# Transposing x for the last residual in the gap before the second norm, and reading the spread norm from PSUM

## The chip, the cores and the metric

The kernel runs on one core of a Trainium2 chip. The metric is the device time of one execution in microseconds (us). Three runs of the kernel before gave 1666.32, 1663.96 and 1669.1 us, so the median is 1666.32 us.

## The reference

One layer of a hybrid backbone works on 512 tokens of width 1024. What matters here lies between the two halves of the layer:

```python
    y, _ = bidir_mix(feats, lg_f, lg_b, ctx_states)
    x = x + g1 * (y.astype(x.dtype) @ w_out)
    x = x + g2 * peer_ffn(modulate(rmsnorm(x, norm2_w), sh2, sc2),
                          peer_w_q, peer_k1, peer_k2, peer_down, peer_up)
    ...
    return rmsnorm(x, norm_f_w)
```

`rmsnorm` divides each token by the root of its mean square, and `modulate` scales and shifts it. `peer_ffn` projects the result h to queries, multiplies them with two sets of 128 keys per head, takes the top 16 of each, the top 16 of their sums, and weights 16 expert rows per head. The x in front of `peer_ffn` is needed twice: for h, and at the very end, where the expert sum is added to it.

## The kernel before, in words

Up to the second norm x is held transposed: `xT` has the width on the partitions, as 8 tiles of 128 by 512 tokens. The attention half ends with the output projection (L641 to L649): TensorE (PE) makes eight PSUM tiles `px`, four at a time, and VectorE (DVE) adds each to `xT` (L650). ScalarE (ACT) squares each result, and DVE adds the squares up into `acc2`, except the last one, which stays alone as `sq` (L651 to L657).

Then comes the norm, with little for PE to do. `meansq` (L176) sums the squares over the partitions by twelve matmuls with one column each, the last four of which need `sq`. `rstd` (L199) takes the root on ACT (`r2`), the reciprocal on DVE, and `spread` makes a diagonal matrix `dg` on DVE and multiplies it with ones on PE, so that PSUM tile `rb` holds the factor of each token on every partition. ACT copies `rb` into the SBUF tile `rs2` (L204).

After that the pools of the first half are closed (`front.close()`), and pools of the second half take their SBUF and their eight PSUM banks. The loop at L684 makes h for each of the eight `xT` tiles: `tmp` = xT * a2x * rs2 on DVE, `hh` = tmp + shift rounded on ACT, `hl` = the rest on DVE, and `hg`, the last 128 tokens unrounded, on ACT. `tmp` has two buffers. `hg` is transposed on PE into `phr` and copied by ACT to `hr` (L691 to L696).

All later products are made by `product` (L698) in three matmuls per tile (`mm3`, lines L73 to L75): of rounded and rest parts. A weight block comes by DMA on SP's queue (`qr` or `dr`), is rounded on ACT (`qh`, `dh`), its rest is made on DVE (`ql`, `dl`), and 24 matmuls follow, into `pq` for a query block (L782) or into `pa` for a block of expert weights (L712). Expert blocks fill PE during the top-k loop (L791): a query block, the scores `pks` (L801), then three or four expert blocks for each half of a head, while DVE finds the maxima. Each of the eight heads ends with one piece of the transposition of `xT`: four PE transposes into `px2`, an ACT copy to `xr`, and a DMA to `x2d` in DRAM (L854 to L859). `finish` (L1021) reads `x2d` at the end of the kernel.

The order in which instructions stand on an engine is made by a scheduler from the program's dependences and its own costs. Each engine then works strictly through its own list. A tile that gets the memory of a closed pool waits until the instructions that still use that memory are done; this holds for PSUM banks and SBUF, and a buffer that a DMA reads is in use until the DMA has landed.

Of the kernel before, what the change touches and what calls it, by code (L numbers as in the profile page):

```python
# [9 lines left out]
F32 = mybir.dt.float32  # L10
# [4 lines left out]
AF = mybir.ActivationFunctionType  # L15
# [3 lines left out]
P = 128  # L19
D = 1024  # L20
KT = 8
L = 512
# [25 lines left out]
def body(nc, tc, a, out, dbg=None):  # L48
    V, S, G, T, Y = nc.vector, nc.scalar, nc.gpsimd, nc.tensor, nc.sync
# [3 lines left out]
    def pool(name, bufs=1, **kw):  # L53
        return tc.tile_pool(name=name, bufs=bufs, **kw)

    def open_pool(name, bufs=1, **kw):
        return es.enter_context(pool(name, bufs, **kw))

    cst = open_pool("cst")
# [5 lines left out]
    def ps(name, tag="ps"):  # L65
        return psum.tile([P, 512], F32, tag=tag, name=name, bufs=banks[tag])
# [17 lines left out]
    ident = cst.tile([P, P], F32, name="ident")  # L84
# [22 lines left out]
    wk = front.enter_context(pool("wk", 2))  # L107
# [4 lines left out]
    def tmp_tile(name, n=L):  # L112
        return wk.tile([P, n], F32, tag="t", name=name, bufs=4)
# [62 lines left out]
    def meansq(pt, terms):  # L176

        nc_ = terms[0].shape[-1] // P
        for i, sq in enumerate(terms):
            for c in range(nc_):  # L180
                T.matmul(pt[:, c:c + 1], sq[:, c * P:(c + 1) * P], onesd, start=(i == 0 and c == 0),
                         stop=(i == len(terms) - 1 and c == nc_ - 1))
# [5 lines left out]
    def inverse_rms(r, pt):  # L188
        S.activation(r, pt[:, :r.shape[-1]], AF.Sqrt, bias=epsc)
        V.reciprocal(r, r)  # L190

    def spread(pb, r, dg):

        nc_ = r.shape[-1]
        V.tensor_tensor(dg.rearrange("p (c j) -> p c j", j=P), ident[:, None, :].to_broadcast([P, nc_, P]),
                        r[:, :, None].to_broadcast([P, nc_, P]), MUL)
        T.matmul(pb[:, :nc_ * P], ones, dg, start=True, stop=True)

    def rstd(dst, pt, pb, dg, name):  # L199
        n = dst.shape[-1]  # L200
        r = cst.tile([P, n // P], F32, name=name)
        inverse_rms(r, pt)
        spread(pb, r, dg)
        S.activation(dst, pb[:, :n], AF.Copy)  # L204
        return dst
# [69 lines left out]
    def group(g, transposed, ctx_cols=None):  # L275
        px, pc = group_start(ctx_cols)
        for kp in range(4):
            group_piece(g, kp, px, pc, transposed, ctx_cols)
            mods_step(2)
        return px, pc  # L280
# [5 lines left out]
    px = [ps(f"px{i}", "px") for i in range(4)]  # L286

    pc2 = ps("pc", "pc")
    pc = [pc2[:, :256], pc2[:, 256:]]
# [123 lines left out]
    px, pc = group(1, False, (0, 512))  # L413
# [35 lines left out]
    for pr in range(2):  # L449
# [9 lines left out]
        for d in range(2):  # L459
# [22 lines left out]
            kn = wk.tile([P, 4, P], F32, name="kn")  # L482
# [61 lines left out]
    px, pc = group(2, True, (0, 512))  # L544
# [6 lines left out]
    px, pc = group(3, False, (0, 512))  # L551
# [13 lines left out]
    px, pc = group(4, True)  # L565
# [21 lines left out]
    for h in range(4):  # L587
# [9 lines left out]
        for b in range(4):  # L597
            psc = ps("psc", "pc")
            T.matmul(psc, rkT[:, h, b * P:(b + 1) * P], rqT[:, h], start=True, stop=True)
            pt = tmp_tile("pt")  # L600
# [5 lines left out]
    for g, tag in ((5, "gqk"), (6, "gv")):  # L606
        gt = mx.tile([P, 4, L], F32, tag=tag, name="gate")
        px, _ = group(g, True)
# [12 lines left out]
    for g, th, tl in ((0, "hch", "hcl"), (1, "hxh", "hxl")):  # L621
        yh = fe.tile([P, 4, L], F32R, tag=th, name="yh")
        yl = fe.tile([P, 4, L], F32R, tag=tl, name="yl")
        for i in range(4):
            h = 4 + i if g == 0 else i
# [9 lines left out]
    x2p = x2s.enter_context(pool("x2p", side="right"))  # L635
    x2d = drp.tile([L // P, P, D], F32, name="x2d")
    xT = x2p.tile([P, KT, L], F32, name="xT")
    Y.dma_start(xT, a["xT"])
    rs2 = x2p.tile([P, L], F32, name="rs2")
    sqs = []  # L640
    for dh in range(2):  # L641
        px = [ps(f"px{i}", "px" if dh else "pc" if i < 2 else "ps") for i in range(4)]
# [5 lines left out]
        for i in range(4):  # L648
            k = 4 * dh + i  # L649
# [8 lines left out]
    show("x2", xT)  # L658
    pt2 = ps("ms2")
    meansq(pt2, sqs)  # L660
    rstd(rs2, pt2, ps("rb"), tmp_tile("dg"), "r2")
    front.close()
    psa = open_pool("psa", space=bass.MemoryType.PSUM)
    pss = ExitStack()
# [16 lines left out]
    tw = qs.enter_context(pool("tw", 2))  # L681
# [10 lines left out]
    for i in range(2):  # L692
        pt = ps("phr", "b")
# [72 lines left out]
    def rows_step(n):  # L766
        for _ in range(n):
            next(rowwise, None)
# [22 lines left out]
    for h in range(H):  # L791
        vv = tw.tile([P, 2, 4, 16], F32, name="vv")
        vi = tw.tile([P, 2, 4, 16], U32, name="vi")
        for half in range(2):
            blk = 2 * h + half
            if blk + 1 < 2 * H:
                query(blk + 1)
            qT = qTs[blk]
            psc = ps("pks", "b")
            for t in range(4):  # L800
                T.matmul(psc[:, t * P:(t + 1) * P], qT[:, t * P:(t + 1) * P], keys[:, blk], start=True, stop=True)  # L801
            sc_ = tw.tile([P, 4, P], F32, name="sc_")
            S.activation(sc_, psc.rearrange("p (t n) -> p t n", t=4), AF.Copy)
            for t in range(4):
                if t < AHEAD[blk]:
                    ahead(1)
                if h:
                    rows_step(DOTS_H // 8)
                s2 = tw.tile([P, P], F32, name="s2")
                V.max(vv[:, half, t, 0:8], sc_[:, t])  # L810
                V.max_index(vi[:, half, t, 0:8], vv[:, half, t, 0:8], sc_[:, t])
                V.match_replace(s2, vv[:, half, t, 0:8], sc_[:, t], NEG)
                V.max(vv[:, half, t, 8:16], s2)
                V.max_index(vi[:, half, t, 8:16], vv[:, half, t, 8:16], s2)
        fi = tw.tile([P, 2, 4, 16], F32, name="fi")
        G.tensor_scalar_mul(fi[:, 0], vi[:, 0], 128.0)
        G.tensor_copy(fi[:, 1], vi[:, 1])
        cs = tw.tile([P, 4, NCAND], F32, name="cs")
        ce = tw.tile([P, 4, NCAND + NC8], F32, name="ce")
        for src, dst, rows in ((vv, cs, ROWS), (fi, ce, ROWS + tuple((r[0], r[1], r[2], NCAND + r[3]) for r in ROWS8))):  # L820
            for a0, na, nb, off in rows:
                o = dst[:, :, off:off + na * nb].rearrange("p t (x y) -> p t x y", x=na)
                G.tensor_tensor(o, src[:, 0, :, a0:a0 + na][:, :, :, None].to_broadcast([P, 4, na, nb]),
                                src[:, 1, :, 0:nb][:, :, None, :].to_broadcast([P, 4, na, nb]), ADD)
        tv = gall[:, :, h]
        ti = tw.tile([P, 4, 16], U32, name="ti")
        for t in range(4):
            s3 = tw.tile([P, NCAND], F32, name="s3")
            V.max(tv[:, t, 0:8], cs[:, t])
            V.max_index(ti[:, t, 0:8], tv[:, t, 0:8], cs[:, t])  # L830
            V.match_replace(s3, tv[:, t, 0:8], cs[:, t], NEG)
            V.max(tv[:, t, 8:16], s3)
            V.max_index(ti[:, t, 8:16], tv[:, t, 8:16], s3)
        G.tensor_tensor(ex[:, :, h], tv, tv[:, :, 0:1].to_broadcast([P, 4, 16]), SUB)
        if h == H - 1:
            S.activation(ex, ex, AF.Exp)

        tf = tw.tile([P, 2, 32, 2], F16, name="tf")
        for half in range(2):
            V.tensor_copy(tf[:, half].rearrange("p (t k) q -> p t k q", t=4),  # L840
                          ti[:, :, 8 * half:8 * half + 8][:, :, :, None].to_broadcast([P, 4, 8, 2]))
        for half, (c0, nc_) in enumerate(((NCAND, NC8), (0, NCAND))):
            ks = slice(8 * half, 8 * half + 8)
            eq = tw.tile([P, 32 * NCAND], F16, name="eq")[:, :32 * nc_]
            V.tensor_tensor(eq.rearrange("p (k c q) -> p k c q", k=32, q=2),
                            ic[:, c0:c0 + nc_].rearrange("p (c q) -> p c q", q=2)[:, None].to_broadcast([P, 32, nc_ // 2, 2]),
                            tf[:, half, :, None, :].to_broadcast([P, 32, nc_ // 2, 2]), ALU.is_equal)
            pe = tw.tile([P, 32 * NCAND], F32, name="pe")[:, :32 * nc_]
            V.tensor_tensor(pe.rearrange("p (t k c) -> p t k c", t=4, k=8), eq.rearrange("p (t k c) -> p t k c", t=4, k=8),
                            ce[:, :, c0:c0 + nc_][:, :, None, :].to_broadcast([P, 4, 8, nc_]), MUL)  # L850
            V.tensor_reduce(eall[:, :, h, ks], pe.rearrange("p (t k c) -> p t k c", t=4, k=8), AX.X, ADD)  # L851
        V.tensor_copy(rows_e[:, 16 * h:16 * h + 16], eall[:, 3, h])

        pt = ps("px2", "b")  # L854
        for k in range(4):
            T.transpose(pt[:, k * P:(k + 1) * P], xT[:, 4 * (h % 2) + k, (h // 2) * P:(h // 2) * P + P], ident)
        xr = tw.tile([P, 512], F32, name="xr")
        S.activation(xr, pt, AF.Copy)
        Y.dma_start(x2d[h // 2, :, 512 * (h % 2):512 * (h % 2) + 512], xr)  # L859
    zs = tq.tile([P, 4, H], F32, name="zs")  # L860
    V.tensor_reduce(zs, ex, AX.X, ADD)
    V.reciprocal(zs, zs)
# [14 lines left out]
    for src, dst in ((eall, eT), (gall, gT)):  # L877
        pt = ps("ptr", "b")[:, :NT]
# [165 lines left out]
    for j in range(NB // 2):  # L1044
        steps = pair_steps(j + 1) if j + 1 < NB // 2 else iter(())
        us, wh, wl = ready.pop(j)
        for x in range(2):
            uh, ul = us[x]
            i = 2 * j + x
            for tt in range(NT // P):  # L1050
# [6 lines left out]
                if j < len(due) and (x or tt):  # L1057
                    k = int(np.ceil((due[j] - done) / (6 - 3 * x - tt)))
# [93 lines left out]
```

## Time and profile before

| | us |
|---|---|
| median of three runs | 1666.32 |
| profiled execution | 1667.1 |
| its span, first to last instruction | 1665.3 |
| PE busy (97% of the span) | 1612.3 |
| DVE busy (76%) | 1272.5 |
| ACT busy (38%) | 633.1 |

The profiled execution's own time is 1.8 us over its span. The page shows the share of each engine, but the stretch of the change is only some 45 of 1665 us. It is read in the timeline of each engine, from 397 us (the end of the output projection) to 442 us (the end of the second set of scores).

### The profile page before, as it was taken

Reading aid. Unit: us, or ns where it says so; the run is one execution under the profiler, and the core shown is the slowest. Engines: PE = TensorE matmul, PEld = TensorE weight load, DVE = VectorE, ACT = ScalarE, POOL = GpSimd, SP = SyncE. Lnnn points to the kernel's source line nnn. Section 1 sums busy time; section 2 is a strip of 40 time slices with the busy share of each in tenths; the row PEclk is TensorE's granted clock in tenths of the full one; section 3 lists DMA queues with packets and bytes.
Section 4 is the critical chain, followed back from the end, with each engine's and each line's share of the span. In section 5 each row is a group of like instructions: output and inputs, shape, how many; then the busy total and the mean of one; then the engine's idle time right before and its main releaser. Section 6 shows DMA issues by size and latency. Waiting matters only on the chain.

```text
span 1665.3 us, 23009 instructions
## 1 busy us (share of the span) xinstructions
PE 1612.3 (97%) x8580; PEld 1380.0 (83%) x8580; DVE 1272.5 (76%) x2178; ACT 633.1 (38%) x851; POOL 456.8 (27%) x413
## 2 busy tenths in 40 slices
PE   5999999999999999999999999999999999999996
PEld 4777785677989999999899999978788888888885
DVE  4665866356678988888788888565888888888886
ACT  4554441334433333333344444432333333333333
POOL 0000101000143333334023322223544445444430
PEclk9999999998999999999999999999999999999999
DMA  8353252153487767667589899999999999999981
GB/s 335 132 178 107 80 166 76 38 189 102 129 288 255 232 223 246 227 205 255 165 295 361 315 339 319 345 375 337 334 382 383 386 382 387 378 383 376 376 318 51
DMA packets 177695, 435.02 MB, mean 261 GB/s; under 512 B 15472, under 2 KB 94320, under 8 KB 174640
## 3 DMA queue, kind: packets, MB, share of 16 engines
q1 hardware_dynamic: 124016, 276.52, 47.6%
q0 software_dynamic: 36864, 134.23, 22.1%
q10 hardware_dynamic: 16704, 22.81, 3.9%
q8 instruction: 67, 1.10, 0.3%
q14 instruction: 44, 0.36, 0.1%
HBM read 381.34 MB, written 52.17 MB: 260 GB/s over the span
## 4 chain that ended last, share of the span: by engine, by line
PE 81%; DVE 14%; issue 2%; ACT 1%; DMA 1%; POOL 0%; SPq 0%; DVEq 0%; ACTq 0%; POOLq 0%
PE po L73 10%; PE po L75 10%; PE po L74 10%; PE pa L73 8%; PE pa L75 7%; PE pa L74 7%; PE px L73 4%; PE px L75 4%; PE px L74 4%; PE pgd L913 3%; DVE dl L705 2%; DVE row L751 1%; PE pq L74 1%; PE pq L73 1%; DVE eall L851 1%
## 5 line engine op out<-in xcount | busy, mean ns | idle before, releaser
L73 PE MATMUL pa<-hh,dh 128*128 128x384 f32 x1024 | 354.4, 346 | 3.2 <-ACT hh L687 2.2
L75 PE MATMUL pa<-hh,dl 128*128 128x384 f32 x1024 | 345.2, 337 | 5.7 <-DVE dl L705 5.6
L74 PE MATMUL pa<-hl,dh 128*128 128x384 f32 x1024 | 344.4, 336 | 0.0
L744 POOL DMA_INDIRECT row<-in_down,rows_e x128 | 176.1, 1376 | 421.2 <-DVE row L751 373.5
L744 POOL DMA_INDIRECT row<-in_up,rows_e x128 | 212.7, 1662 | 219.3 <-DVE og__2888 L759 195.0
L704 ACT ACTIVATE dh<-dr 128x1024 fp32r<-128x1024 f32 x128 | 135.8, 1061 | 307.1 <-PE pa L74 306.1
L705 DVE TENSOR_TENSOR dl<-dr,dh 128x1024 fp32r<-128x1024 f32 x128 | 155.9, 1218 | 78.4 <-ACT dh L704 78.4
L75 PEld LDWEIGHTS pa<-hh,dl 128*128 128x128 f32 x1024 | 193.3, 189 | 8.5 <-DVE dl L705 8.1
L73 PEld LDWEIGHTS pa<-hh,dh 128*128 128x128 f32 x1024 | 193.8, 189 | 6.4 <-ACT hh L687 4.2
L74 PEld LDWEIGHTS pa<-hl,dh 128*128 128x128 f32 x1024 | 193.9, 189 | 1.0 <-DVE hl L688 0.3
L73 PE MATMUL po<-uh,wwh 128*128 128x512 f32 x420 | 166.4, 396 | 7.9 <-ACT wwh L80 4.3
L74 PE MATMUL po<-ul,wwh 128*128 128x512 f32 x420 | 165.3, 394 | 0.0
L759 DVE SCALAR_TENSOR_TENSOR og__2888<-row,wg,og__2888 128x1024 f32<-128x1024 f32 x127 | 162.8, 1282 | 2.6
L75 PE MATMUL po<-uh,wwl 128*128 128x512 f32 x420 | 164.4, 395 | 0.0
L751 DVE SCALAR_TENSOR_TENSOR row<-row,hr 128x1024 f32<-128x1024 f32 x128 | 155.9, 1222 | 6.9 <-DMA row<-in_down,rows_e 6.9
L74 PE MATMUL po<-dl,wwh 128*128 128x512 f32 x348 | 135.4, 389 | 0.0
L73 PE MATMUL po<-dh,wwh 128*128 128x512 f32 x348 | 135.4, 389 | 0.0
L75 PE MATMUL po<-dh,wwl 128*128 128x512 f32 x348 | 135.4, 389 | 0.0
L80 ACT ACTIVATE dh<-dr 128x1024 fp32r<-128x1024 f32 x58 | 61.6, 1062 | 146.7 <-issue 142.9
L80 ACT ACTIVATE wwh<-ae 128x768 fp32r<-128x768 f32 x64 | 54.2, 846 | 158.1 <-DVE ae L1002 136.0
L81 DVE TENSOR_TENSOR wwl<-ae,wwh 128x768 fp32r<-128x768 f32 x64 | 61.3, 958 | 55.8 <-ACT wwh L80 55.8
L73 PEld LDWEIGHTS po<-uh,wwh 128*128 128x128 f32 x420 | 80.1, 191 | 25.5 <-ACT wwh L80 5.6
(438 smaller groups left out, 2926.6 us busy)
## 6 DMA issues: line engine op xcount, KB each, us to landing
dr<-in_downT SPq DMA_DIRECT2D x128, 512.0 KB, 4.7
ur<-in_up SPq DMA_DIRECT2D x70, 512.0 KB, 8.8
dr<-in_up SPq DMA_DIRECT2D x58, 512.0 KB, 9.5
gd<-stg SPq DMA_DIRECT2D x12, 2048.0 KB, 8.9
gt<-gd SPq DMA_DIRECT2D x32, 768.0 KB, 13.0
ad<-at ACTq DMA_DIRECT2D x116, 192.0 KB, 4.1
ae<-ad SPq DMA_DIRECT2D x58, 384.0 KB, 11.4
wm<-in_wmodT SPq DMA_DIRECT2D x32, 512.0 KB, 3.4
```

The source lines that it names most:

```text
L73: T.matmul(o, ah, bh, start=start, stop=False)
L74: T.matmul(o, ah, bl, start=False, stop=False)
L75: T.matmul(o, al, bh, start=False, stop=stop)
L80: hold(S.activation(hi, src, AF.Copy))
L81: hold(V.tensor_tensor(lo, src, hi.bitcast(F32), SUB))
L704: S.activation(rh, r, AF.Copy)
L705: V.tensor_tensor(rl, r, rh.bitcast(F32), SUB)
L744: G.indirect_dma_start(r, None, table, bass.IndirectOffsetOnAxis(rows_e[:, s:s + 1], 0))
L751: pin(V.scalar_tensor_tensor(r, r, 1.0, hr, MUL, MUL, accum_out=ag[:, s_:s_ + 1]))
L759: pin(V.scalar_tensor_tensor(og_, r, w1, og_, MUL, ADD))
L851: V.tensor_reduce(eall[:, :, h, ks], pe.rearrange("p (t k c) -> p t k c", t=4, k=8), AX.X, ADD)
L913: T.matmul(pg[:, t], o2[:, g + t], ow[:, x, g + t], start=(x == 0), stop=(x == 1))
```

## The change

`rs2` is no longer made: `rb` stays in PSUM, and the first multiplication of h (`tmp`) reads it there. The pieces of the transposition of `xT` leave the ends of the heads and stand right behind the norm, all eight of them, before the pools of the first half are closed. Their PSUM tiles are taken in turn from the tags `px` (four banks) and `pc` (two), their `xr` tiles in turn from the tags `kn` and `sw` of the first half's pool `wk` (two buffers each). The pieces with even t are copied by ACT, those with odd t by DVE.

```diff
-    rs2 = x2p.tile([P, L], F32, name="rs2")
...
     pt2 = ps("ms2")
     meansq(pt2, sqs)
-    rstd(rs2, pt2, ps("rb"), tmp_tile("dg"), "r2")
+    r2 = cst.tile([P, L // P], F32, name="r2")
+    inverse_rms(r2, pt2)
+    rs2 = ps("rb")
+    spread(rs2, r2, tmp_tile("dg"))
+
+    for dh in range(2):
+        for t in range(L // P):
+            pt = ps("px2", "pc" if t % 2 else "px")
+            for k in range(4):
+                T.transpose(pt[:, k * P:(k + 1) * P], xT[:, 4 * dh + k, t * P:t * P + P], ident)
+            xr = wk.tile([P, 512], F32, tag="sw" if t % 2 else "kn", name="xr")
+            if t % 2:
+                V.tensor_copy(xr, pt)
+            else:
+                S.activation(xr, pt, AF.Copy)
+            Y.dma_start(x2d[t, :, 512 * dh:512 * dh + 512], xr)
     front.close()
...
-        pt = ps("px2", "b")
-        for k in range(4):
-            T.transpose(pt[:, k * P:(k + 1) * P], xT[:, 4 * (h % 2) + k, (h // 2) * P:(h // 2) * P + P], ident)
-        xr = tw.tile([P, 512], F32, name="xr")
-        S.activation(xr, pt, AF.Copy)
-        Y.dma_start(x2d[h // 2, :, 512 * (h % 2):512 * (h % 2) + 512], xr)
```

The lines behind the change move down by 14 (to the heads' end) and then by 7, so that L695 becomes L709 and L705 becomes L719.

The scheduler gives another order. On PE, from the norm on, this stood before (`ms` is the mean square, the number behind a name tells tiles apart):

```order
L181 MATMUL ms_2775<-onesd,sq 128x1 x4
L197 MATMUL rb<-dg,ones 128x512
L73 MATMUL pa<-hh,dh 128x384 x2
L695 MATMUL phr<-ident,hg 128x128 x2
L74 MATMUL pa<-hl,dh 128x384
L75 MATMUL pa<-hh,dl 128x384
L73 MATMUL pa<-hh,dh 128x384
L74 MATMUL pa<-hl,dh 128x384 x2
L75 MATMUL pa<-hh,dl 128x384 x2
```

And this stands there now, from the fourth piece of the transposition on (12 transposes of the first three pieces stand ahead of it):

```order
L669 MATMUL px_2818<-ident,xT 128x128 x3
L181 MATMUL ms_2774<-onesd,sq 128x1 x4
L669 MATMUL px_2818<-ident,xT 128x128
L669 MATMUL px_2826<-ident,xT 128x128 x4
L669 MATMUL px_2834<-ident,xT 128x128 x4
L669 MATMUL px_2842<-ident,xT 128x128 x4
L669 MATMUL px_2850<-ident,xT 128x128 x2
L197 MATMUL rb<-dg,ones 128x512
L669 MATMUL px_2850<-ident,xT 128x128 x2
L709 MATMUL phr<-ident,hg 128x128 x8
L73 MATMUL pq<-hh,qh 128x512
L74 MATMUL pq<-hl,qh 128x512
```

Between `rb` and the first query block there were 25 matmuls of two expert blocks, mixed with the transposes of `hg`. Now all eight transposes of `hg` stand directly behind `xT`'s, then two whole query blocks, then `pks`, and the first expert block behind them.

On DVE, from the last addition to `xT` on, this stood before:

```order
L650 SCALAR_TENSOR_TENSOR xT<-px_2640,modx,xT 128x512
L190 RECIPROCAL r_2790<-r_2790 128x4
L195 TENSOR_TENSOR dg<-ident,r_2790 128x512
L705 TENSOR_TENSOR dl<-dr,dh 128x1024
L686 SCALAR_TENSOR_TENSOR tmp<-xT,a2x,rs_2497 128x512 x2
L705 TENSOR_TENSOR dl<-dr,dh 128x1024
```

And this now:

```order
L649 SCALAR_TENSOR_TENSOR xT<-px_2639,modx,xT 128x512
L672 COPY xr<-px_2802 128x512
L672 COPY xr<-px_2818 128x512
L190 RECIPROCAL r_2787<-r_2787 128x4
L195 TENSOR_TENSOR dg<-ident,r_2787 128x512
L719 TENSOR_TENSOR dl<-dr,dh 128x1024
L672 COPY xr<-px_2834 128x512
L672 COPY xr<-px_2850 128x512
L719 TENSOR_TENSOR dl<-dr,dh 128x1024
L700 SCALAR_TENSOR_TENSOR tmp<-xT,a2x,rb 128x512 x2
```

Two copies have come ahead of the reciprocal, and two ahead of the first `tmp`; the last two write into the buffers of the first two.

On SP's queue this stood before:

```order
L245 DMA wr<-in_wout 128x1024
L701 DMA qr<-in_wq 128x1024 x2
L701 DMA dr<-in_downT 128x1024 x5
L701 DMA qr<-in_wq 128x1024 x2
L701 DMA dr<-in_downT 128x1024 x3
```

And this now:

```order
L245 DMA wr<-in_wout 128x1024
L715 DMA qr<-in_wq 128x1024 x2
L715 DMA dr<-in_downT 128x1024
L675 DMA x2d<-xr 128x512 x4
L715 DMA dr<-in_downT 128x1024
L675 DMA x2d<-xr 128x512 x4
L715 DMA dr<-in_downT 128x1024 x3
```

The eight writes to `x2d` stand among the first loads of expert weights, and the second load waits in the queue behind the first four of them.

## Rows read from the trace of the kernel before

**Rows 1.** The page's part 1: busy us, share of the span, instructions.

```profile
PE 1612.3 (97%) x8580; PEld 1380.0 (83%) x8580; DVE 1272.5 (76%) x2178; ACT 633.1 (38%) x851; POOL 456.8 (27%) x413
```

**Rows 2.** Windows: length, then PE, PEld, DVE, ACT, POOL busy, clock, DMA, GB/s.

```profile
550.00:650.00 100.00, 99.11 (x551) 94.03 (x550) 86.50 (x282) 33.55 (x48) 36.63 (x53) 1.00 0.71 240
```

**Rows 3.** Waits of PE, 425-500, 760-860, 860-1666 us: total, times, longest.

```profile
PE pa L75 <- DVE dl L705: 2.7, 1, 2.7
...
PE ptr L880 <- DVE eall L851: 1.1, 1, 1.1
...
PE po L73 <- ACT wwh L80: 4.3, 1, 4.3
```

**Rows 4.** Timeline of PE in the gap: start, us, line, operation, count [idle before].

```profile
399.20 1.03 PE L181 MATMUL ms<-onesd,sq 128*128 128x1 f32 x8
401.52 2.08 PE L197 MATMUL rb<-dg,ones 128*128 128x512 f32 x2 [1.29 <-DVE dg L195]
405.84 1.01 PE L73 MATMUL pa<-hh,dh 128*128 128x384 f32 x2 [2.24 <-ACT hh L687]
```

**Rows 5.** Timeline of DVE in the gap.

```profile
397.70 0.75 DVE L650 SCALAR_TENSOR_TENSOR xT<-px,modx,xT 128x512 f32<-128x512 f32 x1 [0.58 <-PE px L75]
400.78 0.69 DVE L195 TENSOR_TENSOR dg<-ident,r 128x512 f32<-128x512 f32 x1
404.26 1.41 DVE L686 SCALAR_TENSOR_TENSOR tmp<-xT,a2x,rs 128x512 f32<-128x512 f32 x2 [1.00 <-ACT rs L204]
414.42 0.75 DVE L686 SCALAR_TENSOR_TENSOR tmp<-xT,a2x,rs 128x512 f32<-128x512 f32 x1
415.93 0.75 DVE L686 SCALAR_TENSOR_TENSOR tmp<-xT,a2x,rs 128x512 f32<-128x512 f32 x1
```

**Rows 6.** Timeline of ACT in the gap.

```profile
398.48 0.63 ACT L653 ACTIVATE sq<-xT 128x512 f32<-128x512 f32 x1 [2.08 <-DVE xT L650]
400.27 0.26 ACT L189 ACTIVATE r<-ms,epsc 128x4 f32<-128x4 f32 x1 [1.16 <-PE ms L181]
403.63 0.60 ACT L204 ACTIVATE rs<-rb 128x512 f32<-128x512 f32 x1 [1.63 <-PE rb L197]
417.35 0.39 ACT L689 ACTIVATE hg<-tmp,modx 128x128 f32<-128x128 f32 x1
418.15 0.60 ACT L696 ACTIVATE hr<-phr 128x512 f32<-128x512 f32 x1 [0.42 <-PE phr L695]
```

**Rows 7.** Timeline of PE: a piece of the transposition, and what follows it.

```profile
458.58 0.60 PE L856 MATMUL px<-ident,xT 128*128 128x128 f32 x4
458.94 0.48 PE L73 MATMUL pq<-hh,qh 128*128 128x512 f32 x1
459.25 0.40 PE L74 MATMUL pq<-hl,qh 128*128 128x512 f32 x1
```

**Rows 8.** Tiles xr, x2d and, in 397 to 420 us, dr: min/median/max.

```profile
L858 ACT ACTIVATE xr<-px x8: 587/590/592, 459.9 to 790.1; 128x512 f32<-128x512 f32 x8
DMA to landing us min/median/max: 2.3/4.2/4.8
...
DMA to landing us min/median/max: 3.1/3.2/5.6
```

**Rows 9.** Windows as in Rows 2, where TensorE's clock fell and rose.

```profile
401.00:402.00 1.00, 0.48 (x1) 0.48 (x2) 0.47 (x1) 1.00 (x1) 0.00 (x0) 0.50 0.69 238
411.00:412.00 1.00, 1.00 (x7) 0.95 (x6) 0.90 (x3) 0.00 (x0) 0.00 (x0) 0.92 0.00 0
```

**Rows 10.** Timeline of PE: an expert block, a query block's rest, scores, next block.

```profile
431.44 0.44 PE L73 MATMUL pa<-hh,dh 128*128 128x384 f32 x1
...
435.71 0.39 PE L73 MATMUL pq<-hh,qh 128*128 128x512 f32 x1
...
440.62 1.05 PE L801 MATMUL pks<-keys,qT 128*128 128x128 f32 x8
441.43 0.42 PE L73 MATMUL pa<-hh,dh 128*128 128x384 f32 x1
```

## The prediction

> **What bounds the kernel now.** I read the page's part 1 first: PE is busy for 1612.3 us, 97% of the span, DVE for 76%, ACT for 38% [rows 1]. What changes the time is what changes PE's stream: matmul time on it, or holes in it. Then the windows of the top-k loop, from which the change takes the pieces of the transposition: in a stretch of 100 us PE is busy for 99.11 and DVE for 86.50 [rows 2], so there a microsecond off PE is a microsecond off the end. PE's waits in and behind that loop are few; the largest are 2.7 us for `dl` early on, 1.1 us for `eall` at the loop's end and 4.3 us for `wwh` in the last stage [rows 3]. Last the timelines of PE, DVE and ACT around the norm [rows 4 to 6], where PE has its largest hole: from about 400.2 us to 405.84 us it runs only `rb`. The reader is to see two things there. PE takes up expert blocks (`pa`) at 405.84, as soon as the first `hh` exists, while DVE and ACT go on making h until 418; so the eleven microseconds in which h is made are hardly a hole for PE. And the chain sq, ms, r, reciprocal, dg, rb, rs, tmp runs link by link: whatever is put between two links delays all behind.
>
> **What leaves the top-k loop.** A piece is four transposes: they start at 458.58 and the query block behind them at 458.94, so 0.36 us; the next matmul follows after 0.31 instead of some 0.23 (21 matmuls from 435.71 to 440.62), so 0.43 us in all [rows 7, 10]. Eight pieces cost 3.5 us. The last stands ahead of the wait for `eall` at the loop's end, which would hide most of it [rows 3], so seven count: -3.0 us. The eight ACT copies (0.59 us each [rows 8]) and the eight DMAs go as well, at no gain: ACT is busy for 33.55 of 100 us there [rows 2]. The copy `rs` (0.60 us [rows 6]) goes from the chain. A `tmp` that reads PSUM I cost as one that reads SBUF: the addition to `xT` reads PSUM with as many elements in 0.75 us, `tmp` takes 0.75 [rows 5].
>
> **What the gap gets.** Now the new chain, step by step, on the clock of the profiled execution.
> - The first eight matmuls of ms end at 399.20, where `sq`'s begin [rows 4]. The first piece then needs 0.60 us until its end [rows 7], so its ACT copy runs from 399.8 to 400.4. This copy stands ahead of `sq` on ACT, so `sq` starts at 400.4, not 398.48: +1.9. From `sq` to r takes 1.8 us as before (398.48 to 400.27 [rows 6]), so r starts at 402.2.
> - On DVE the copy of the fourth piece stands ahead of the reciprocal, and its last transpose stands behind ms: some 402.5. The trace shows no such DVE copy; its bounds are ACT's 0.59 [rows 8] and DVE's 0.75 for three operands [rows 5]. I take 0.7, since the engine is the same as in the second: 403.2. Reciprocal (0.2, the time between r's end and dg's start) and dg (0.69 [rows 5]) follow: 404.1, where it was 401.47.
> - rb takes 2.08 us at the low clock, as it did [rows 4]; I keep that. 406.2, and with the last two transposes 406.5.
> - The buffers of `xr` are two for each tag. Copies five to eight write into those of one to four, so each waits until a DMA to DRAM has landed. Behind DVE's two wait the second `dl` and every `tmp`; behind ACT's two the second `dh` and every `hh`. The fourth DMA is issued at 403.3. Landing lies between 2.3 and 4.8 us in the trace; the 4s fall in the loop, where loads and row reads crowd the queues, and the loads in this very gap landed in 3.2 at the median [rows 8]. I take 3.2: 406.5, the same moment at which the eighth piece is ready. Its copy ends at 407.2.
> - The first `tmp` lies in SBUF that the `xr` buffers used. The built program makes it wait for all eight DMAs. The eighth is issued at 407.3 and lands at 410.5. So the first `tmp` starts at 410.5 instead of 404.26: +6.2. With 2.3 per landing it is 409.5, with 4.8 it is 413.5.
>
> The Trainium skill (DMA: Bandwidth & Descriptors, on the fixed cost) says that a DMA costs about 2.0 us whatever its size, most of it waiting for the receipt of the write at the target, and less under light load. By that the landing could be 2.0 and the first `tmp` at 409.2, which would lower the sum by 1.3 us. The lowest landing in the trace, 2.3, is near it and the median of 4.2 far off [rows 8].
>
> **What happens to PE.** `phr` has the PSUM bank of `rb`, which is now read until the eighth `tmp`. All eight `phr` transposes stand ahead of the query blocks on PE, and no expert block stands ahead of them any more. So PE does nothing while h is made.
> - Eight `tmp`: the first two together, the third about 0.9 us after them (it needs the buffer of the first, behind one `hl`), then one each 1.51 us (414.42 to 415.93 [rows 5]); the eighth starts 9.9 us after the first. From there `hg` is done in 1.8 (415.93 to 417.74) and `hr`, for which the first query block waits, in 0.6 more [rows 6]. The query block starts at 410.5 + 12.3 = 422.8.
> - From there to the end of the second `pks` PE has three query blocks, two sets of scores and three expert blocks. In before this same set, all of it, was done at 441.43. By rows: 24 matmuls of an expert block 4.27 us (431.44 to 435.71), a query block 24/21 of 4.91, so 5.61, scores 0.81 [rows 10]. Sum 12.8 + 16.8 + 1.6 = 31.3.
> - The clock was granted at 0.50 (1.2 GHz) from 401 us on, after PE had run only one-column matmuls and then stood, and was back (2.4 GHz) in the window 411 to 412, some 5.3 us after it had steady work [rows 4, 9]. After a far longer stand the query block starts at the low level: half of 5.3, so 2.7 us. With a quicker return it is 1.7.
> - End: 422.8 + 31.3 + 2.7 = 456.8 instead of 441.43, so +15.4.
>
> Sum: 15.4 - 3.0 = **+12.4 us**. The profiled execution's 1667.1 becomes 1679.5; its distance to the median (0.8) goes off, so 1678.7. Nothing behind gives this back: the loop, the gates and the last stage are PE's work in line, and what PE has still to do is the same.
>
> **Rivals.**
> - *Faster, as a filled gap would be.* The place is PE's list: were expert blocks still taken up at about 405.84, then all of +15.4 but the chain's own shift would go, and if that shift too were hidden (landings under 1 us) only -3.0 and the `rs` copy's 0.6 would stay: 1662.7. It decides the matter from the point at which a `pa` can start before the last `tmp`. The transposes of `hg` ahead of it and `rb`'s bank speak against it. 6%.
> - *Only the bank counts.* If the landings cost nothing, the first `tmp` follows the eighth copy, at 407.2, and the sum is 3.3 less: +9.1, 1675.4. If also the copies were hidden and the first `tmp` came at 404.3, it is 6.2 less: +6.2, 1672.5. What speaks for it is that dr loads landed quickly here [rows 8]; against, that two rounds of landings stand one behind the other. 14%.
> - *Later waits take it up.* PE's three waits of 2.7, 1.1 and 4.3 us [rows 3] could vanish if DVE and ACT, which are fed earlier relative to PE's expert blocks than before, run ahead. That is 12.4 - 8.1, so +4.3: 1670.6. Against it: these waits hang on work that itself starts from the late scores, and the last on PE's own results. 12%.
> - *Slow landings.* At 4.8 us per round, +15.4: 1681.7. 13%.
> - My forecast, with its sizes off by up to 3 us: 55%.
>
> **How the numbers follow.** About 0.3%, or 5 us, is what a measurement can tell from no change. Slower by more than that (over 1671.3) are my forecast, the slow landings, nearly all of the second rival and a part of the third: 84%. Within it are most of the third, the better part of the first (its 1662.7 is 3.6 us off) and the low end of the second: 13%. Faster by more, if the first also saves some of PE's old hole: 3%. My forecast's own range is 1675 to 1682. The range for 8 in 10 goes down to 1670, where the third rival ends, and up to 1683, with slow landings and a slow clock.
>
> **What will show it.** In the changed kernel's timelines: `sq` near 400.4; `dg` ending near 404; DVE waiting for a DMA ahead of its third and fourth copy and ahead of the first `tmp`, which starts near 410; PE empty from some 407 to some 422 but for transposes; no `pa` before the first `pks`; the clock at half when the query block starts; the second set of scores ended near 457. I am wrong if PE runs products before the eighth `tmp`, if the first `tmp` starts before 408, or if the second scores end before 450. If these three hold and the time is still under 1672, the loss was given back later, and the waits of PE behind 457 have to show where.

## The result, and the profile after

The changed kernel takes 1676.96 us (median of six runs, 1676.01 to 1678.12), the kernel before 1664.18 us beside it (six runs, 1662.48 to 1669.1). The ratio is 1.0071, with an interval of 1.0061 to 1.0082: slower by some 12 us (10 to 14). Forecast were 1678.7 us and +12.4.

The page's part 1 of the changed kernel, as in [rows 1]:

```profile
PE 1610.2 (96%) x8580; PEld 1380.7 (82%) x8580; DVE 1274.5 (76%) x2182; ACT 631.3 (38%) x846; POOL 450.7 (27%) x413
```

PE's work is the same (1610.2 us against 1612.3), and the span is longer, 1674.2 us against 1665.3. So the loss is holes in PE. The difference of the two spans, 8.9 us, is not the size of the loss: each is one execution, and stretches with the same instructions differ between executions. I therefore measure each kernel from its own end of the output projection, the start of its first `ms` on PE. The first row here is that mark in the kernel before, in its timeline of PE (start, us, line, operation, count [idle before]):

```profile
397.50 1.73 PE L181 MATMUL ms<-onesd,acc 128*128 128x1 f32 x15
```

The timeline of PE in the changed kernel, from the same mark on, answers to [rows 4, 10]:

```profile
395.44 1.84 PE L181 MATMUL ms<-onesd,acc 128*128 128x1 f32 x16
...
401.80 1.12 PE L197 MATMUL rb<-dg,ones 128*128 128x512 f32 x2
402.76 0.38 PE L669 MATMUL px<-ident,xT 128*128 128x128 f32 x2
420.70 1.94 PE L709 MATMUL phr<-ident,hg 128*128 128x128 f32 x8 [17.56 <-DVE tmp L700]
422.48 0.80 PE L73 MATMUL pq<-hh,qh 128*128 128x512 f32 x1
...
435.53 1.05 PE L815 MATMUL pks<-keys,qT 128*128 128x128 f32 x8
436.34 0.42 PE L73 MATMUL pa<-hh,dh 128*128 128x384 f32 x1
...
454.53 1.05 PE L815 MATMUL pks<-keys,qT 128*128 128x128 f32 x8
```

PE stands for 17.56 us and is released by a `tmp`, the last one. Its first product comes 27.0 us after the mark, where the kernel before had its first `pa` after 8.3 us (405.84 - 397.50 [rows 4]). The second scores start 59.1 us after the mark, before 43.1 (440.62 - 397.50 [rows 10]): +16.0. No expert block runs before the first scores.

DVE in the same stretch, as in [rows 5]:

```profile
398.25 0.69 DVE L672 COPY xr<-px 128x512 f32<-128x512 f32 x1 [1.86 <-PE px L669]
...
401.05 0.69 DVE L195 TENSOR_TENSOR dg<-ident,r 128x512 f32<-128x512 f32 x1
...
402.80 1.28 DVE L672 COPY xr<-px 128x512 f32<-128x512 f32 x2
406.65 1.22 DVE L719 TENSOR_TENSOR dl<-dr,dh 128x1024 fp32r<-128x1024 f32 x1 [2.57 <-ACT dh L718]
409.72 1.41 DVE L700 SCALAR_TENSOR_TENSOR tmp<-xT,a2x,rb 128x512 f32<-128x512 f32 x2 [1.85 <-DMA x2d<-xr]
...
419.81 0.75 DVE L700 SCALAR_TENSOR_TENSOR tmp<-xT,a2x,rb 128x512 f32<-128x512 f32 x1
```

The first `tmp` is released by a DMA to `x2d`, 14.3 us after the mark (before 6.8). The third and fourth copy (402.80) hardly waited for a landing. ACT's timeline, as in [rows 6]:

```profile
398.31 0.62 ACT L652 ACTIVATE sq<-xT 128x512 f32<-128x512 f32 x1
...
400.07 0.26 ACT L189 ACTIVATE r<-ms,epsc 128x4 f32<-128x4 f32 x1 [0.66 <-PE ms L181]
...
405.56 1.06 ACT L718 ACTIVATE dh<-dr 128x1024 fp32r<-128x1024 f32 x1 [3.04 <-DMA dr<-in_downT]
```

The norm's links on ACT are where the forecast had them, and `dh` waits for its load. SP's queue, where the writes and the loads are issued:

```profile
398.44 2.84 SPq L675 DMA_DIRECT2D x2d<-xr  x4
401.32 0.43 SPq L715 DMA_DIRECT2D dr<-in_downT  x1
401.85 2.94 SPq L675 DMA_DIRECT2D x2d<-xr  x4
404.85 3.38 SPq L715 DMA_DIRECT2D dr<-in_downT  x3
```

The last of the eight writes is issued near 404.4, and the `tmp` that it holds up starts at 409.72, so its landing took up to 5.3 us. Two things stand beside it in the queue: a load of 512 KB between the two rounds of writes (401.32), and three such loads behind the eighth. The one in front delays the second round: from 402.70 to 404.50 the DMA engines move packets of 4 KB on average, which are rows of that load, although the fifth write, whose rows have 2 KB, was issued at 401.85.

```profile
DMA packets 89, 0.36 MB, mean 203 GB/s; under 512 B 0, under 2 KB 0, under 8 KB 89
```

The same load also holds DVE up by itself: its `dh` starts at 405.56, the second `dl` waits 2.57 us for that `dh`, and `tmp` stands behind `dl`. The landing adds the last 1.85 us. What the three loads behind add no run shows. The windows (length, then PE, PEld, DVE, ACT, POOL busy, clock, DMA share, GB/s) show the DMA engines full from 404 to 408, and the clock at its lower level from about 406 to 426:

```profile
404.00:406.00 2.00, 0.00 (x0) 0.00 (x0) 0.08 (x1) 0.44 (x1) 0.00 (x0) 0.95 0.96 374
406.00:408.00 2.00, 0.00 (x0) 0.00 (x0) 1.22 (x1) 0.61 (x1) 0.00 (x0) 0.50 1.14 313
...
424.00:426.00 2.00, 2.00 (x6) 1.59 (x5) 0.00 (x0) 0.00 (x0) 0.00 (x0) 0.50 0.00 0
426.00:428.00 2.00, 2.00 (x9) 1.63 (x8) 0.00 (x0) 0.00 (x0) 0.00 (x0) 0.93 0.00 0
550.00:650.00 100.00, 99.69 (x551) 94.26 (x550) 84.68 (x278) 33.17 (x47) 32.98 (x51) 1.00 0.70 236
```

PE's waits in the stretches of [rows 3] (total, times, longest) are nearly those of before:

```profile
PE pa L75 <- DVE dl L719: 2.0, 1, 2.0
...
PE ptr L887 <- DVE eall L865: 1.6, 1, 1.6
...
PE po L73 <- ACT wwh L80: 4.3, 1, 4.3
```

They were 2.7, 1.1 and 4.3. What was lost by the second scores is given back only in the top-k loop: the last scores start 384.6 us after the mark instead of 372.1, +12.4. So the loop returned 3.5.

### The profile page after: what moved, and what is told of

The parts are those of the page before. It is cut to its first block, busy times and chain, and to the rows that moved or that the text cites. A ratio compares the mean times of both kernels' runs of the same rounds, so it can differ in the third digit from the quotient of the medians.

```text
span 1674.2 us, 23011 instructions
## 1 busy us (share of the span) xinstructions
PE 1610.2 (96%) x8580; PEld 1380.7 (82%) x8580; DVE 1274.5 (76%) x2182; ACT 631.3 (38%) x846; POOL 450.7 (27%) x413
## 4 chain that ended last, share of the span: by engine, by line
PE 79%; DVE 15%; DMA 2%; issue 2%; ACT 1%; SPq 0%; POOL 0%; DVEq 0%; ACTq 0%; POOLq 0%
PE po L73 10%; PE po L75 10%; PE po L74 10%; PE pa L73 7%; PE pa L75 7%; PE pa L74 7%; PE px L73 4%; PE px L75 4%; PE px L74 4%; PE pgd L920 3%; DVE dl L719 2%; DVE row L765 1%; PE pq L73 1%; PE pq L74 1%; PE pq L75 1%
## 5 line engine op out<-in xcount | busy, mean ns | idle before, releaser
L758 POOL DMA_INDIRECT row<-in_down,rows_e x128 | 172.6, 1348 | 445.5 <-DVE row L765 364.8
L719 DVE TENSOR_TENSOR dl<-dr,dh 128x1024 fp32r<-128x1024 f32 x128 | 156.0, 1218 | 82.3 <-ACT dh L718 81.1
L80 ACT ACTIVATE wwh<-ae 128x768 fp32r<-128x768 f32 x64 | 54.1, 846 | 158.9 <-DVE ae L1009 137.1
```

The source lines that it names most:

```text
L80: hold(S.activation(hi, src, AF.Copy))
L719: V.tensor_tensor(rl, r, rh.bitcast(F32), SUB)
L758: G.indirect_dma_start(r, None, table, bass.IndirectOffsetOnAxis(rows_e[:, s:s + 1], 0))
```

## The experiments

Three theories were set against each other at first. **A**: two causes add up; a norm that stays in PSUM keeps PE empty while h is made, and the landings of `x2d` delay h. **B**: only the landings count. **C**: only the norm held in PSUM counts. The table gathers what all kernels showed: from each one's profile the starts of the first `tmp`, the first product (`pa` or `pq`), and the second and the last `pks`, in us after its own mark; then the ratio to the kernel before, beside which it ran (five rounds for the experiments).

| kernel | tmp | product | 2nd scores | last scores | ratio and interval |
|---|---|---|---|---|---|
| before | 6.8 | 8.3 | 43.1 | 372.1 | 1 |
| changed | 14.3 | 27.0 | 59.1 | 384.6 | 1.0071 [1.0061, 1.0082] |
| psum_only | 5.5 | 19.6 | 50.9 | 379.0 | 1.0045 [1.0030, 1.0060] |
| gap_only | 14.1 | 15.8 | 50.4 | 375.8 | 1.0016 [1.0004, 1.0027] |
| no_landing | 9.1 | 22.5 | 54.1 | 380.1 | 1.0039 [1.0024, 1.0054] |
| copy_no_landing | 9.1 | 10.6 | 45.2 | 369.6 | 0.9995 [0.9981, 1.0009] |
| bank_px | 5.2 | 19.3 | 50.9 | 380.9 | 1.0055 [1.0037, 1.0073] |
| new_pool | 6.2 | 7.8 | 42.8 | 373.3 | 1.0004 [0.9993, 1.0014] |
| whole_new_pool | 14.1 | 15.6 | 49.8 | 375.3 | 1.0018 [1.0009, 1.0027] |
| no_pieces | 6.8 | 8.3 | 43.4 | 369.0 | 0.9965 [0.9953, 0.9978] |
| pieces_mix | 8.8 | 10.7 | 44.7 | 369.0 | 0.9984 [0.9970, 0.9997] |
| pieces_act | 7.1 | 9.8 | 45.6 | 371.3 | 0.9994 [0.9982, 1.0006] |

**psum_only**: the second edit alone, on the kernel before.

```diff
-    rstd(rs2, pt2, ps("rb"), tmp_tile("dg"), "r2")
+    r2 = cst.tile([P, L // P], F32, name="r2")
+    inverse_rms(r2, pt2)
+    rs2 = ps("rb")
+    spread(rs2, r2, tmp_tile("dg"))
```

> The kernel before with one part of the change: rb is not copied, the first multiplication reads it in PSUM; the pieces of the transposition stay in the top-k loop. Theory A (two causes that add up: a norm that is held in PSUM keeps PE empty while h is made, and the landings of the x2d writes delay h): the first tmp comes 6.2 us after the output projection's end (6.8 before, the copy being gone), the first query block 12.8 us after it as in the changed kernel, and the second scores end 52 us after the projection (43.9 before, 59.5 changed). No piece leaves the loop, so +8.0 us: 1672.2, ratio 1.0048. Theory B (only the landings count; the expert blocks that PE does not run in the gap it runs later, at no loss): 1663.6, ratio 0.9996. Theory C (only the held norm counts): some 12 us more, 1676, ratio 1.007.

Measured 1674.65 us against 1665.89, ratio 1.0045. One fewer instruction on the chain, and 7.5 us lost. Its timeline of PE:

```profile
403.47 1.48 PE L197 MATMUL rb<-dg,ones 128*128 128x512 f32 x2 [1.29 <-DVE dg L195]
417.28 1.94 PE L697 MATMUL phr<-ident,hg 128*128 128x128 f32 x8 [12.34 <-issue]
419.06 0.79 PE L73 MATMUL pq<-hh,qh 128*128 128x512 f32 x1
```

h is made earlier than before (first `tmp` after 5.5 us instead of 6.8), and PE still stands for 12.34 us. The profile names no releaser for this wait ("issue": none that it shows), but it ends when the eighth `tmp` ends, at 417.2. The first `hg`, all that the first `phr` transpose needs of h, was there at 406.8. B falls.

**gap_only**: the first edit alone; `rb` is copied to `rs2` as before.

```diff
-    r2 = cst.tile([P, L // P], F32, name="r2")
-    inverse_rms(r2, pt2)
-    rs2 = ps("rb")
-    spread(rs2, r2, tmp_tile("dg"))
+    rs2 = x2p.tile([P, L], F32, name="rs2")
+    rstd(rs2, pt2, ps("rb"), tmp_tile("dg"), "r2")
```

> The changed kernel with the other part alone: all pieces of the transposition in the gap, but rb copied to SBUF as before. Theory A: the first tmp still waits for the eighth write, 13.9 us after the projection's end (+7.2), but PE takes up expert blocks with the first hh; second scores at 43.9 + 7.2 = 51.1, less 3.0 for the pieces gone from the loop: +4.2 us, 1668.4, ratio 1.0025. Theory B (landings alone): as the changed kernel, 1677, ratio 1.0077. Theory C (held norm alone): the copies' 1.5 us less 3.0: 1662.7, ratio 0.999.

Measured 1668.93 us, ratio 1.0016. PE takes up expert blocks 1.6 us after the first `tmp` again, as in the kernel before, but that `tmp` waits for a landing. DVE's timeline:

```profile
411.14 1.22 DVE L717 TENSOR_TENSOR dl<-dr,dh 128x1024 fp32r<-128x1024 f32 x1 [2.68 <-ACT dh L716]
413.96 1.42 DVE L698 SCALAR_TENSOR_TENSOR tmp<-xT,a2x,rs 128x512 f32<-128x512 f32 x2 [1.60 <-DMA x2d<-xr]
```

C, by which the time had to return to before's, falls too. SP's queue has the order of the changed kernel, and here the profile gives the landings: of the first four writes (issued 402.82 to 405.34), of the load behind them (405.71) and of the fifth write (406.24); us, minimum, median and maximum of each.

```profile
DMA to landing us min/median/max: 2.0/2.2/2.4
...
DMA to landing us min/median/max: 4.3/4.3/4.3
...
DMA to landing us min/median/max: 4.5/4.5/4.5
```

The fifth write lands 0.7 us after the load in front of it.

**no_landing**: the changed kernel, but `x2d` is written from `xT` as it lies, so no `xr` buffer waits for a DMA (the output differs by that). **copy_no_landing** is gap_only with the same line.

```diff
-            Y.dma_start(x2d[t, :, 512 * dh:512 * dh + 512], xr)
+            Y.dma_start(x2d[t, :, 512 * dh:512 * dh + 512], xT[:, 4 * dh + t])
```

> The changed kernel, but the writes to x2d read xT itself (512 numbers a partition, not transposed), which stays in place until the end of top-k: transposes and copies to xr run as before, and no buffer waits for a landing. Theory A: the first tmp follows the copies, 8.3 us after the projection's end (13.9 changed); PE stays empty until the last hg; second scores at 8.3 + 12.8 + 32.9 = 54.0, +10.1, less 3.0: +7.1 us, 1671.3, ratio 1.0043. Theory B (landings alone): 1662.7, ratio 0.999. Theory C (held norm alone): as the changed kernel, 1677, ratio 1.0077.

> Both causes taken away: pieces in the gap, rb copied to SBUF, writes to x2d that read xT itself (not transposed). Theory A: the first tmp 8.9 us after the projection's end (+2.1 for the pieces and copies in the chain), PE takes up expert blocks at once, 3.0 less in the loop: -0.9 us, 1663.3, ratio 0.9995. A third cause (the copies on ACT and DVE beside h, or the low clock that stays longer) would show as a time clearly over 1664.2: some 1667 or more.

Measured 1673.29 us (1.0039) and 1664.64 us (0.9995). The difference is 5.0 us at the second scores (59.1 - 54.1) and 5.2 in the other pair (50.4 - 45.2). DVE in no_landing waits 0.24 us for the first of the two `dh`, and goes from the last copy straight to the first `tmp`:

```profile
404.86 1.22 DVE L719 TENSOR_TENSOR dl<-dr,dh 128x1024 fp32r<-128x1024 f32 x1 [0.24 <-ACT dh L718]
406.00 0.68 DVE L672 COPY xr<-px 128x512 f32<-128x512 f32 x1
406.79 1.41 DVE L700 SCALAR_TENSOR_TENSOR tmp<-xT,a2x,rb 128x512 f32<-128x512 f32 x2
```

The edit does more than end the wait for landings. Writes that need no copy leave earlier, seven of the eight before the mark. So the second load of expert weights is issued 1.3 us after the mark instead of 5.9, and the second `dl` now stands behind the first two `tmp`. The 5 us are therefore the price of the landings and of the load between them together; no run parts the two.

So A holds, with that load counted to the landings. What remained was why a norm held in PSUM stops PE. The prediction blamed the one bank that `rb` shares with `phr`. The other reading is that the wait belongs to the closed pool as a whole.

**bank_px**: psum_only with `rb` in another bank of the old pool.

```diff
-    rs2 = ps("rb")
+    rs2 = ps("rb", "px")
```

> The kernel before, with the norm read from PSUM as in psum_only, but rb lies in one of the four banks of tag px, which none of the tiles phr, pq and pa of the second half uses. Bank theory (the prediction's words: PE waits because phr has the bank of rb): the bank of phr is free, so expert blocks start at the first hh and the time is that of the kernel before less the rs copy, ratio 0.9995, first matmul of a product near 8 us after the projection's end. Pool theory (every PSUM tile of the second half waits for the last reader of any tile of the closed pool): no difference from psum_only, ratio 1.0045, first product near 19.6 us.

Measured 1674.89 us against 1664.68, ratio 1.0055. PE waits as long as in psum_only:

```profile
402.75 1.12 PE L197 MATMUL rb<-dg,ones 128*128 128x512 f32 x2 [1.29 <-DVE dg L195]
416.23 1.94 PE L697 MATMUL phr<-ident,hg 128*128 128x128 f32 x8 [12.35 <-issue]
```

And it waits for the same thing, the eighth `tmp` on DVE, which ends at 416.13:

```profile
415.38 0.75 DVE L688 SCALAR_TENSOR_TENSOR tmp<-xT,a2x,rb 128x512 f32<-128x512 f32 x1
```

The bank theory falls.

**new_pool**: `rb` is read from PSUM too, but from the pool of the second half, which is opened ahead of it (`fps` holds the first half's PSUM pool alone). The lines that open `psa` and `psm` move up to the dots.

```diff
-    rstd(rs2, pt2, ps("rb"), tmp_tile("dg"), "r2")
+    r2 = cst.tile([P, L // P], F32, name="r2")
+    inverse_rms(r2, pt2)
+    fps.close()
...
+    rs2 = psum.tile([P, 8, P], F32, tag="g", name="rb", bufs=2)[:, :4].rearrange("p k c -> p (k c)")
+    spread(rs2, r2, tmp_tile("dg"))
```

> The norm is read from PSUM, but the first half's PSUM pool is closed right after the mean square and rb is taken from the second half's pool (its tag g, not used until the gates). Pool theory: phr, pq and pa wait for the root's reading of ms alone, expert blocks start at the first hh, and the time is that of the kernel before less 0.6 us for the rs copy: ratio 0.9995, first product near 8 us after the projection's end. Held-norm theory (a norm that DVE reads from PSUM keeps PE empty wherever it lies): as psum_only, ratio 1.0045, first product near 19.6.

Measured 1665.45 us, ratio 1.0004. PE takes up `pa` as in the kernel before:

```profile
400.88 2.04 PE L198 MATMUL rb<-dg,ones 128*128 128x512 f32 x2 [1.39 <-DVE dg L196]
404.52 0.69 PE L74 MATMUL pa<-hh,dh 128*128 128x384 f32 x1 [1.59 <-ACT hh L691]
```

A norm in PSUM costs nothing that these runs can tell when it doesn't hold the old pool. **whole_new_pool** is the whole change with the same edit.

> The whole change, with rb in the second half's PSUM pool as in new_pool. Pool theory: what is left is the landings' share, as in gap_only, ratio 1.0016, second scores near 51 us after the projection's end. Held-norm theory: as the changed kernel, ratio 1.0071, second scores near 60.

Measured 1668.05 us, ratio 1.0018: the pool's part is gone, the part of the landings and their load is left, as in gap_only.

**no_pieces** measures the loop's term: the pieces leave the heads of the kernel before, and `x2d` is written from `xT` as it lies. The writes, which need no copy now, don't stay in the heads either: they are issued from 368.0 to 398.5 us.

```diff
-        pt = ps("px2", "b")
-        for k in range(4):
-            T.transpose(pt[:, k * P:(k + 1) * P], xT[:, 4 * (h % 2) + k, (h // 2) * P:(h // 2) * P + P], ident)
-        xr = tw.tile([P, 512], F32, name="xr")
-        S.activation(xr, pt, AF.Copy)
-        Y.dma_start(x2d[h // 2, :, 512 * (h % 2):512 * (h % 2) + 512], xr)
+        Y.dma_start(x2d[h // 2, :, 512 * (h % 2):512 * (h % 2) + 512], xT[:, 4 * (h % 2) + h // 2])
```

> The kernel before without the eight pieces of the transposition: x2d is written from xT as it lies, by the same eight DMAs in the heads, so the output differs by that. It measures the loop's term by itself. The prediction's price: seven pieces of 0.43 us, -3.0 us, ratio 0.9982; by the marks of the changed kernel -3.5, ratio 0.9979. Rival: the gain is taken up by the loop's and the last stage's waits, ratio 1.0000.

Measured 1659.24 us, ratio 0.9965, so -5.8 us with an interval of -7.8 to -3.7, more than either theory gave. From the second to the last scores its trace is shorter by 3.4 us (325.6 against 329.0). A part of that is one wait, PE's for `dl` from 425 to 770 us (total, times, longest). In the kernel before:

```profile
PE pa L75 <- DVE dl L705: 5.0, 6, 2.7
```

And in no_pieces:

```profile
PE pa L75 <- DVE dl L705: 3.0, 6, 2.2
```

These are 2.0 us less. Whether the writes that left the loop have a part in this no run shows, and where the other 2.4 us of the median come from stays open. From the first `pgd` to the end, which the edit doesn't touch, the twelve profiled executions take 835.8 to 839.5 us, and this one is the shortest.

**pieces_mix** and **pieces_act** use what was learnt. PSUM changes hands right behind the root, as in new_pool; `rb` is copied to `rs2`; the pieces, as four of double size, take PSUM tiles from the tag `g` and `xr` tiles from the row buffers of the second half. Those are wanted only by the first gather, so nothing waits for a landing. In pieces_act all four copies are ACT's.

```diff
+    for t in range(L // P):
+        pt = psum.tile([P, 8, P], F32, tag="g", name="px2", bufs=2)
+        for k in range(KT):
+            T.transpose(pt[:, k], xT[:, k, t * P:t * P + P], ident)
+        xr = ga.tile([P, D], F32, tag="row", name="xr", bufs=6)
+        if t % 2:
+            V.tensor_copy(xr, pt.rearrange("p k c -> p (k c)"))
+        else:
+            S.activation(xr, pt.rearrange("p k c -> p (k c)"), AF.Copy)
+        Y.dma_start(x2d[t], xr)
```

> Another way to the same end: the kernel before, its PSUM pools changed right behind the root, the norm copied to rs2 as before, and the eight pieces made there as four of double size: their PSUM tiles from the second half's tag g, their xr tiles in the six row buffers of the second half, which are not wanted before the first gather. So nothing of the closed pools is held and no buffer waits for a landing. Copies of 1024 columns in turn by ACT and DVE. Theory (a closed pool that is held and the landings are what the change lost, and the loop gains 3 to 5.8 us as in no_pieces): expert blocks start some 2 us later than before, near 10 us after the projection's end, and 1 to 4 us are gained, ratio 0.9976 to 0.9994. Rival (any work put between the norm and h costs as much there as the loop gives back, as copy_no_landing may be read): ratio 1.0000.

> As pieces_mix, with all four copies on ACT (some 1.1 us each, by dh's 1061 ns for as many columns): two stand ahead of the first hh and two ahead of the second. Theory: expert blocks start some 2 to 3 us later than before and h's second tile 4 us later; ratio 0.9980 to 1.0000, not better than pieces_mix. Rival: ratio 1.0000 or over.

Measured 1662.86 us (0.9984) and 1663.92 us (0.9994) against 1665.77. pieces_mix is faster than the kernel before by 2.7 us, with an interval of 0.5 to 5.0, and so beats both. pieces_act is not told from no change. The timeline of PE in pieces_mix:

```profile
397.92 1.48 PE L692 MATMUL px<-ident,xT 128*128 128x128 f32 x8 [0.35 <-ACT r L190]
399.19 1.92 PE L198 MATMUL rb<-dg,ones 128*128 128x512 f32 x2
...
402.77 2.07 PE L692 MATMUL px<-ident,xT 128*128 128x128 f32 x16 [0.34 <-ACT xr L697]
405.58 0.62 PE L74 MATMUL pa<-hh,dh 128*128 128x384 f32 x2 [0.74 <-ACT hh L703]
```

The transposes lie in PE's hole, as the changed kernel meant them to. One window of pieces_mix, in the columns of [rows 2]:

```profile
408.00:410.00 2.00, 0.81 (x4) 0.34 (x3) 2.00 (x4) 1.83 (x4) 0.00 (x0) 1.00 0.42 164
```

Expert blocks start 2.4 us later than before (10.7 against 8.3), but the second scores only 1.6. What speaks for the clock as the reason is that it is granted in full at 408 to 410, where the same window of the kernel before shows half; no run tests it alone:

```profile
408.00:410.00 2.00, 2.00 (x8) 2.00 (x8) 1.87 (x4) 1.17 (x3) 0.00 (x0) 0.50 0.63 238
```

## Why the prediction was right

The time, its side and its mechanism came as forecast: PE empty while h is made, h late by the landings, and no gain behind that covers it. The cause that it gave for the empty PE, one shared bank, was too narrow. Of the signs that it named only one is missing: DVE had next to no wait for a DMA ahead of its third and fourth copy. By the prediction's steps, its times turned into us after the mark (minus 397.50):

- *Loop, -3.0.* 3.5 by the marks (from the second to the last scores 329.0 us before, 325.5 now); 3.0 to 4.8 in the eight kernels that have no pieces in the loop, while the three experiments that keep them lie between 0.9 under and 1.5 over the kernel before. The price per piece held; the lower waits for `dl` were not in it.
- *`sq` at 400.4, r at 402.2* (2.9 and 4.7): 2.9 and 4.6. *DVE's copy 0.7*: 0.69. *dg's end at 404.1* (6.6): 6.3.
- *rb 2.08 us at the low clock*: wrong, 1.12 [rows 4]. PE had transposes and `ms` without a pause ahead of it, and the clock was still granted at 1.00. So rb ended 7.5 us after the mark instead of 8.7.
- *A landing of 3.2 in each of two rounds*: wrong in both, and the errors nearly cancel. In the first round the third and fourth copy began 7.4 us after the mark and ended at 8.6, so the fourth write, issued by 401.3, had landed by about 403.4: some 2 us, as in gap_only (2.0 to 2.4). The eighth took up to 5.3. The step that I didn't take was to look at the load that SP issues between the two rounds: the second round stood in line behind it. All eight landings of [rows 8], the one of 2.3 too, are from the heads, so none of them had this queue around it. The Trainium skill (DMA: Bandwidth & Descriptors, on the fixed cost) has about 2.0 us fixed, in a fit to DMAs that GpSimd issues, and adds the bytes at 436 GB/s, which the prediction left out; by that 256 KB take 2.6 us, an estimate from the page. The first round lies somewhat under it and the second far over it, with a DMA share of 0.96 to 1.14 from 404 to 408.
- *First `tmp` +6.2*: +7.5 (14.3 against 6.8), so 1.3 late.
- *First query block 12.3 us after it*: 12.8. *Three query blocks, two scores and three expert blocks in 31.3, and 2.7 for the clock*: from the first `pq` to the end of the second scores 32.9 instead of 34.0. The clock was back near 426.3 (0.93 in the window 426 to 428), 3.8 us after the first `pq` and 5.6 after the first `phr`: the `phr` transposes ahead of the query block, which the prediction left out of its path, took 1.8 us of the low stretch. Half of 3.8 is 1.9 us; for the 1.7 of a quicker return the prediction names no row.
- *+15.4 at the second scores*: +16.0. *+12.4 in all*: +12.4 at the last scores, and 10 to 14 by the times. That it fits to 0.1 us is luck: the first `tmp` was 1.3 late and the way to the query block 0.5 longer, the stretch from the first `pq` on was 1.1 shorter and the loop gave 0.5 more.
- *Slips in its sums*: by its own terms landings of 2.0, 2.3 and 4.8 put the first `tmp` at 409.3, 409.6 and 413.7, not 409.2, 409.5 and 413.5. Nothing hangs on it.
- *"`phr` has the PSUM bank of `rb`"*: wrong as a cause, right in its effect. bank_px moved `rb` to another bank and PE waited as long; new_pool took it out of the closed pool and the wait was gone. `phr`, the first PSUM tile of the second half that PE writes there, waits for the last reader of the first half's pool, whichever bank that reader's tile has. The general rule on closed pools, as told for the kernel before, held; the prediction narrowed it to one bank. Whether `pq` and `pa` would wait as long no trace shows, as they stand behind `phr` on PE. That order goes with the hold: in new_pool `pa` and `phr` are mixed again as before.

Of the rivals, the filled gap (-3.6 us) came near only in a kernel that holds neither the pool nor its buffers: pieces_mix, with -2.7. That only the bank counts (+9.1 or +6.2) is close to no_landing (+6.5 us), a kernel that had to be made first. The later waits took up nothing: 2.0, 1.6 and 4.3 us against 2.7, 1.1 and 4.3. The slow landings came in one round only.

By single causes the loss comes apart as follows, at the second scores: the held pool 59.1 - 49.8 = 9.3 us (changed against whole_new_pool), the landings and the load between them 5.0, and the copies and transposes in the chain some 2 (45.2 - 43.1 in copy_no_landing). Sum 16.3, measured 16.0. The parts depend a little on each other: the held pool alone costs 7.8 (50.9 - 43.1, psum_only). The loop's 3.5 goes off.

## What to carry to other kernels

When memory passes from one stage's pool to the next, find the last instruction that still reads anything in the old pool: it dates the first write into the next stage's memory (here `phr` on PE for PSUM, and `tmp` on DVE for SBUF), however free its own bank is. Reading a value straight from PSUM to save a copy can so cost many times the copy. Work moved into a hole belongs in memory that the next stage doesn't inherit, and its DMAs are priced with the loads that stand around them in the queue, those in front first.

## What the runs showed of the hardware

- In gap_only writes of 256 KB landed in 2.0 to 2.4 us, and in 3.6 to 4.9 once a load of 512 KB, which itself took 4.3, had been issued in front of them on the same queue. In the changed kernel the DMA engines' share was about 1 at that time.
- `tmp` took 0.75 us with the norm read from PSUM (changed kernel) as with the norm read from SBUF [rows 5].
- The same `rb` (two matmuls) took 1.10 to 1.13 us in the five kernels that have transposes of `xT` between the mark and the end of `ms`. Without them it took 2.08 in the kernel before and in no_pieces, 2.04 in new_pool, 1.48 in psum_only and 1.12 in bank_px, with the same PE work ahead of it. (In pieces_mix and pieces_act, with eight transposes behind `ms`, it took 1.92 and 1.91.) From 4.0 to 5.0 us after the mark the granted clock was 0.50 in the kernel before and 1.00 in bank_px. So the clock's fall from the upper to the lower level came more than a microsecond earlier in some executions than in others.
- A copy of 128 by 512 from PSUM by DVE took 0.69 us, by ACT 0.59 to 0.60 us.
